# Hymba step: the scan's half of the output projection as 2x2x2 block products, with the factors of the scan's outputs built behind each group's norm

## The chip, the cores and the metric

The kernel runs on one core of a Trainium2 chip. The metric is the time of one execution in device microseconds (us). The engines are named as the profile names them: PE (TensorE, matrix products), DVE (VectorE), ACT (ScalarE), POOL (GpSimd) and SP (SyncE, which issues the DMAs). A line number L1040 is a line of the kernel that the row belongs to.

## What is computed

One step of a decoder layer with 1024 channels over T = 1088 tokens (1024 of a prompt, and 8 sequences of 8). The part that the change touches is the mixer and its output projection:

```python
h = rmsnorm(x, g_mix_pre) * (1 + scale_m) + shift_m
proj = h @ w_in
sc_b, sc_c, sc_x, z, xbc, dt_raw = jnp.split(proj, idx, axis=-1)
...
y_sc = sc_b * uc
...
yg = (y_ssd * jax.nn.silu(z)).reshape(bsz, L, SSM_GROUPS, SSM_WIDTH // SSM_GROUPS)
y_ssd = rmsnorm(yg, 1.0).reshape(bsz, L, SSM_WIDTH) * ssm_norm_g
mix = jnp.concatenate([y_sc, y_ssd], axis=-1) @ w_out
x = x + gate_m * rmsnorm(mix, g_mix_post)
```

`uc` is the causal convolution of `sc_c * sc_x`; `y_ssd` is the output of a scan in four groups of 256 channels. So `w_out` has 2048 rows: 1024 for the short convolution's half (`y_sc`) and 1024 for the scan's half (`y_ssd`). After the mixer comes a feed-forward block, which the change leaves alone.

## The kernel before, in words

**Numbers.** Every fp32 matrix is held as a sum of two reduced-precision parts, hi (a cast on ACT) and lo (value minus hi, a subtraction on DVE). A product is three matmuls: hi by hi, hi by lo, lo by hi. `split` (L298 cast, L299 subtraction) does this for a whole row of 1088 tokens, `part` (L1039, L1040) for a block.

**Layout.** Activations lie with channels on the 128 partitions and the 1088 tokens along the row. A row tile is 128 x 1088, 557 KB. A scan group g has two such tiles, `y[0]` and `y[1]`.

**Block products.** Where the kernel multiplies blockwise it cuts both factors 2x2: seven products of blocks in place of eight, after sums and differences of blocks of both factors. `unit` (L1082 on) issues the seven in the order 1, 5, 6, 3, 7, 2, 4. For each it queues its matmuls (`product`, L1078 to L1080) into a PSUM tile `pm` for the first half of tokens (q = 0) and `pz` for the second, then takes the sum out with ACT (`nc.scalar.copy`, L1093) where it opens an output, or DVE (an addition, L1095) where it adds to one. Product 6 adds on top of product 1 in the same PSUM tile, and product 3 on top of product 5, so each must wait until the copy of the earlier sum has been made. A unit of the short convolution has 7 x 24 = 168 matmuls of 272 columns. Such units make the short convolution's input columns (`sc_unit`), and the down projection of the feed-forward block.

**The order of the work.** Program order is written out by hand, with generators that are advanced between steps: `between={n: [gen]}` of a unit advances `gen` once behind its n-th product; `merge(a, b, ratio)` advances b by `ratio` steps for each step of a. A layer then decides from the program order and the buffers where an instruction stands in each engine's queue; each engine runs its queue in order. What matters here is this sequence:

1. The scan of group 3 (`ssd`, to about 450 us). Beside it run the gates and norms of groups 0 and 1 as side work, `merge(..., 1.67)`.
2. The late gates of groups 2 and 3 (`gate_late`, L1165, 470 to 515 us).
3. Twelve units of the short convolution, three for each of four pairs of channel tiles: two input columns' units (`cc`, `cx`), then the convolution of the pair on DVE (L1209, L1210, L422 to L429), then the third unit (`cb`). Unit 3, from about 554 us, is the third unit of the first pair; unit 4 is the first of the second pair. Norms of groups 2 and 3 are advanced between the products of these units.
4. The scan's half of the output projection (770 to 867 us), the short convolution's half behind it.

**The norm of a scan group** (`norm`, L913) computes sums of squares (ACT squares, PE sums), scales the two row tiles on DVE (L939), and then splits each tile: hi goes into a new row buffer, lo stays in place, and both go to DRAM (`y_out`, L948 to L950, tensors `y_d`). For groups 0 and 1 the row buffers come from `fm_row`, a pool with eight of them; for groups 2 and 3 from `sx_row` (L1177):

```python
pap, psx, psy = (pool(left, n, b) for n, b in (("pap", 2), ("psx", 1), ("psy", 1)))
```

So `psx` has a single buffer.

**The scan's half before** (L1277 to L1297) is a plain product. Sixteen row tiles (hi and lo of 8) are loaded into `fx`, `btp` and `h2p`; for each of 4 x 2 column tiles of the weights and each of three pieces of the tokens (512, 304, 272) eight k-tiles of three matmuls are summed (L334 to L336), 576 matmuls in all, and ACT copies the sum into the accumulators `acc`.

Of the kernel before, what the change touches and what calls it, by code (L numbers as in the profile page):

```python
# [9 lines left out]
F32 = mybir.dt.float32  # L10
# [6 lines left out]
P = 128  # L17
D = 1024
# [15 lines left out]
def hymba_step(ctx, tc, i, o):  # L34
# [877 lines left out]

    def norm(g, y, new_sq, new):  # L913

        ps = pz()
        sq = []

        def sums(c):
            for j in range(3):
                mm(ps[:, 3 * c + j:3 * c + j + 1], sq[c][:, 0, j * P:(j + 1) * P], ones[:, 0:1],  # L920
                   start=(c == 0 and j == 0), stop=(c == 2 and j == 2))

        for c, (c0, n) in enumerate(CH):
            q = new_sq()
            sq.append(q)
            if n < 384:
                nc.gpsimd.memset(q[:, 0, n:384], 0.0)
            for m in range(2):
                nc.scalar.square(q[:, m, :n], y[m][:, c0:c0 + n])
            nc.vector.tensor_tensor(q[:, 0, :n], q[:, 0, :n], q[:, 1, :n], op=add)  # L930
            sums(c)
            yield
        r = rsqrt_of(ps[:, 0:9], 2 * P)
        yield
        for c, (c0, n) in enumerate(CH):
            rs = spread(r[:, 3 * c:3 * c + 3], n)
            for m in range(2):
                v = y[m][:, c0:c0 + n]
                nc.vector.scalar_tensor_tensor(v, v, sng[:, 2 * g + m:2 * g + m + 1], rs, op0=mult, op1=mult)  # L939
# [27 lines left out]
    def fm_row():  # L967
        return fmp.tile([P, T], F32, tag="fm", name=nm("nr"))

    def blend(a, b, na, nb):  # L970
# [19 lines left out]
    for g in range(4):  # L990
        if g < 3:
            side = group_tiles(g + 1, tl[g + 1])
            if g > 0:
                side = blend(side, ada_steps(g), 12, 9)
        else:
            gates, norms = zip(*((gate(h, tl[h][:2]), norm(h, tl[h][:2], lambda: gz([P, 2, 384]), fm_row))
                                 for h in range(2)))
            side = itertools.chain(gates[0], norms[0], gates[1], load_next(), norms[1])
        run(merge(ssd(g, *tl[g], load_later if g == 3 else None), side, (0.67, 1.17, 1.17, 1.67)[g]))
    pre_scale("A_f", 4, gpre1)  # L1000
# [36 lines left out]

    def part(hi, lo, v, eng=None):
        nc.scalar.copy(hi, v)  # L1039
        (eng or nc.vector).tensor_tensor(lo, v, hi, op=sub)  # L1040

    def combos_w(w, cols, eng=nc.gpsimd):
# [39 lines left out]
    def unit(W, X, nk, qs, out, first=True, between={}, blocks_=QS, queue=in_order):  # L1082
# [3 lines left out]
        for n, (p, b, new, i, h, opens) in enumerate(ORDER):  # L1086
            for q in qs:
                if new:
                    B[b, q] = (pm, pz)[q]()
                ps = B[b, q][:, :blocks_[q][1]]  # L1090
                queue(product, ps, W[p], X[q][p], nk, new, p in (3, 2, 4))
                if first and opens:
                    nc.scalar.copy(out(q, i, h), ps)  # L1093
                else:
                    nc.vector.tensor_tensor(out(q, i, h), out(q, i, h), ps, op=add)  # L1095
            for gen in between.get(n, ()):
# [101 lines left out]
    for pr in range(4):  # L1198
# [77 lines left out]

    first = []  # L1277
    for k in range(KT):
        v = [(fx, btp, h2p)[(k > 3) + (k > 5)].tile([P, T], F32R, tag="bt" if k in (4, 5) else "fm", name=nm("hb"))
             for _ in range(2)]  # L1280
        first.append(v)
    for cols in (slice(0, 512), slice(512, T)):
        for k in range(KT):
            for e in range(2):
                nc.sync.dma_start(first[k][e][:, cols].bitcast(F32), y_d[8 + k][:, e, cols])
    for mp in range(4):
        for m, (wh, wl) in enumerate(load_cols(w_out, mp * 256, 2, D)):
            for c0, n in OC:
                ps = pm()
                acc3(ps, n, [(wh[:, k, :], wl[:, k, :], first[k][0][:, c0:c0 + n], first[k][1][:, c0:c0 + n])  # L1290
                             for k in range(KT)])
                nc.scalar.copy(acc_at(2 * mp + m, c0, n), ps[:, :n])
        if mp == 0:
            while kept:
                y_out(*kept.pop(0))
        if mp == 2:
            in_order(conv_state, nsc, 8, 2, o["scc_p"], o["scc_s"])  # L1297


    def out_split(c):  # L1300
        c0, n = OC[c]
        terms = []
        for k in range(KT):
            if c < 2:
                hb = ((fa if k < 4 else fb) if c == 0 else fx).tile([P, 2, n], F32R, tag="fm", name=nm("hb"))
            elif k % 2 == 0:
                hb2 = bt_([P, 2, 2, n], F32R)
# [331 lines left out]
    def combos_d(g, mp, eng):  # L1639
        nk = len(g)  # L1640
        raw = raws_d.pop(0) if raws_d else raw_d(g, mp)
        A = raw.rearrange("p (k j) (i c) -> p i j k c", j=2, i=2)
        a11, a12, a21, a22 = (A[:, m, j] for m in range(2) for j in range(2))
        W = {}


        pair = [in_turn(w_from).tile([P, 2, 2, 2, P], F32R, tag="wc", name=nm("wd")) for _ in range(4)]

        def parts_(p, b):
            n = (1, 5, 6, 3, 7, 2, 4).index(p)  # L1650
            t = pair[n // 2][:, n % 2]
            part(t[:, 0], t[:, 1], b)
            W[p] = [[t[:, s, k] for k in range(nk)] for s in range(2)]

        parts_(1, a11)
        parts_(4, a22)
        eng.tensor_tensor(a22, a21, a22, op=add)
        parts_(5, a22)
        eng.tensor_tensor(a21, a11, a21, op=sub)
        eng.tensor_tensor(a11, a22, a11, op=sub)  # L1660
        parts_(6, a11)
        parts_(2, a12)
        eng.tensor_tensor(a12, a12, a11, op=sub)
        parts_(3, a12)
        parts_(7, a21)
        return W

# [128 lines left out]
```

## Time and profile before

| | |
|---|---|
| runs | 1731.94, 1732.16, 1736.8 us; median 1732.16 |
| the profiled execution | 1732.75 us, span from the first to the last instruction 1731.0 us |
| granted PE clock, mean over the span | 0.990 |
| busy: PE, DVE, ACT, POOL | 97%, 66%, 45%, 11% of the span |
| DMA | 256.37 MB, mean 148 GB/s |

How to read it: the busy share of PE is that of a queue with work in it; matmuls are pipelined, and the end of one is modelled. So the time that a stretch of matmuls needs is read from its length and its count, not from the sum of their durations. A row of the windows view gives a stretch's length, then each engine's busy time with its number of instructions, the granted PE clock, the busy share of the DMA engines and GB/s. A row of the timeline gives start, duration, engine, line, operation, output, inputs and, in brackets, how long the engine sat idle before it and what released it.

### The profile page before, as it was taken

The page shows a single profiled execution, that of the slowest core. Times are in us where ns is not written, and L with a number is a line of the kernel's source. Part 1 is how long each engine was busy: PE and PEld are TensorE (multiplying, and loading weights), DVE is VectorE, ACT ScalarE, POOL GpSimd, SP SyncE. Part 2 cuts the span into 40 slices and gives each one's busy share as a digit, 9 for nine tenths or more (in the row PEclk, how much of TensorE's full clock was granted, in tenths as well). Part 3 has the DMA queues.
Part 4 walks back from the last instruction along what each step waited for, and adds up shares of the span by engine and source line. Part 5 has one row for each costly group of instructions (what it writes and reads, how often), then busy time and mean ns, then how long its engine had stood idle before and what let it go on. Part 6 is the DMA issues. An engine that isn't in the chain of part 4 may idle for free. (4 is left out here: it accounts for less than half of the span.)

```text
span 1731.0 us, 31270 instructions
## 1 busy us (share of the span) xinstructions
PE 1682.0 (97%) x12604; PEld 1600.0 (92%) x12604; DVE 1147.9 (66%) x2194; ACT 770.9 (45%) x1571; POOL 185.7 (11%) x277
## 2 busy tenths in 40 slices
PE   5999999999999999999999999999999999999997
PEld 4898888899999999998989999999999999999987
DVE  5588677777798776661037779666666658588734
ACT  3457454657544433322226676444444446422222
POOL 2110001000001000000000000122222200122112
PEclk9999999999999999999999999999999999999999
DMA  9201344442322522348275643334433438865523
GB/s 321 73 21 30 113 152 151 148 131 77 109 69 77 177 70 74 113 165 301 69 255 183 195 134 140 121 140 142 147 131 140 148 123 312 314 230 198 203 92 134
DMA packets 159624, 256.37 MB, mean 148 GB/s; under 512 B 10578, under 2 KB 123394, under 8 KB 157943
## 3 DMA queue, kind: packets, MB, share of 16 engines
q1 hardware_dynamic: 159190, 253.19, 42.9%
q8 instruction: 99, 1.62, 0.4%
q10 hardware_dynamic: 288, 1.18, 0.2%
q14 instruction: 47, 0.38, 0.1%
HBM read 184.63 MB, written 69.71 MB: 147 GB/s over the span
## 5 line engine op out<-in xcount | busy, mean ns | idle before, releaser
L312 DVE TENSOR_TENSOR wl<-raw,wh 128x512 fp32r<-128x512 f32 (+1 forms) x87 | 61.3, 729 | 100.3 <-ACT wh L311 89.2
L334 PE MATMUL pm<-h,wh 128*128 128x384 f32 (+1 forms) x342 | 115.1, 337 | 0.1
L335 PE MATMUL pm<-h,wh 128*128 128x384 f32 (+1 forms) x342 | 114.9, 336 | 0.0
L336 PE MATMUL pm<-h,wl 128*128 128x384 f32 (+1 forms) x342 | 114.3, 335 | 0.0
L336 PE MATMUL pm<-hb,wl 128*128 128x512 f32 (+2 forms) x320 | 107.3, 337 | 2.1 <-DVE wl L312 2.1
L311 ACT CAST wh<-raw 128x512 fp32r<-128x512 f32 (+1 forms) x89 | 56.4, 665 | 116.2 <-PE pm L335 68.2
L335 PE MATMUL pm<-hb,wh 128*128 128x512 f32 (+2 forms) x320 | 107.4, 337 | 0.0
L334 PE MATMUL pm<-hb,wh 128*128 128x512 f32 (+2 forms) x320 | 105.8, 338 | 1.0 <-ACT wh L311 1.0
L1039 ACT CAST wd<-raw 128x256 fp32r<-128x256 f32 x112 | 42.9, 406 | 96.1 <-PE pz L1080 33.6
L1040 DVE TENSOR_TENSOR fs<-f,fs 128x576 fp32r<-128x576 f32 (+2 forms) x76 | 52.9, 710 | 25.3 <-ACT fs L1039 24.5
L336 PEld LDWEIGHTS pm<-hb,wl 128*128 128x128 f32 x320 | 60.8, 190 | 7.6 <-DVE wl L312 2.4
L334 PEld LDWEIGHTS pm<-h,wh 128*128 128x128 f32 x342 | 65.5, 191 | 1.9 <-issue 0.9
L335 PEld LDWEIGHTS pm<-h,wh 128*128 128x128 f32 x342 | 65.3, 191 | 1.4 <-issue 0.7
L334 PEld LDWEIGHTS pm<-hb,wh 128*128 128x128 f32 x320 | 60.3, 190 | 6.8 <-ACT wh L311 1.2
L336 PEld LDWEIGHTS pm<-h,wl 128*128 128x128 f32 x342 | 65.2, 191 | 1.3 <-issue 1.0
L1078 PE MATMUL pz<-fc,wd 128*128 128x288 f32 x224 | 66.2, 295 | 0.0
L1080 PE MATMUL pz<-fc,wd 128*128 128x288 f32 x224 | 66.0, 295 | 0.0
L1079 PE MATMUL pz<-fc,wd 128*128 128x288 f32 x224 | 65.9, 294 | 0.0
L335 PEld LDWEIGHTS pm<-hb,wh 128*128 128x128 f32 x320 | 60.8, 190 | 5.2
L1078 PE MATMUL pm<-fc,wd 128*128 128x256 f32 x224 | 63.3, 283 | 1.4 <-DVE facc L1095 1.4
L1040 DVE TENSOR_TENSOR wd<-raw,wd 128x256 fp32r<-128x256 f32 x112 | 54.4, 494 | 14.6 <-ACT wd L1039 14.2
L1080 PE MATMUL pm<-fc,wd 128*128 128x256 f32 x224 | 63.1, 282 | 0.3 <-DVE wd L1040 0.3
(5568 smaller groups left out, 6203.2 us busy)
## 6 DMA issues: line engine op xcount, KB each, us to landing
raw<-in_w_in SPq DMA_DIRECT2D x48, 512.0 KB
wa<-in_w_ada SPq DMA_DIRECT2D x32, 512.0 KB
raw<-in_w_out SPq DMA_DIRECT2D x32, 512.0 KB
f_d<-fs SPq DMA_DIRECT2D x28, 576.0 KB
f_d<-fs SPq DMA_DIRECT2D x30, 512.0 KB
raw<-in_w_gate SPq DMA_DIRECT2D x28, 512.0 KB
raw<-in_w_up SPq DMA_DIRECT2D x28, 512.0 KB
y_d<-y SPq DMA_DIRECT2D x26, 544.0 KB
```

Of the source, the lines that this page charges most:

```text
L311: (nc.gpsimd.tensor_copy if hi_eng else nc.scalar.copy)(wh, raw)
L312: (eng or nc.vector).tensor_tensor(wl, raw, wh, op=sub)
L334: mm(ps[:, :n], wh, xh, start=(first and j == 0), stop=False)
L335: mm(ps[:, :n], wh, xl, start=False, stop=False)
L336: mm(ps[:, :n], wl, xh, start=False, stop=(last and j == end))
L1039: nc.scalar.copy(hi, v)
L1040: (eng or nc.vector).tensor_tensor(lo, v, hi, op=sub)
L1078: mm(ps, W[0][k], X[0][k], start=(start and k == 0), stop=False, skip_group_check=True)
L1079: mm(ps, W[0][k], X[1][k], start=False, stop=False, skip_group_check=True)
L1080: mm(ps, W[1][k], X[0][k], start=False, stop=(stop and k == nk - 1), skip_group_check=True)
```

## The change

The scan's half of the output projection becomes eight units of block products: two pairs of scan groups (groups 0 and 1, groups 2 and 3) by four pairs of column tiles of the weights, each 7 products x 12 matmuls of 272 columns, 672 matmuls in all. The second pair adds to the accumulators with DVE, where the first opens them with ACT. Each unit's weights are cut and combined (`combos_p`, shared now with the down projection) with sums on DVE for the first pair and on POOL for the second.

The block sums of the scan's outputs are made once, behind each group's norm. `factors_out` makes seven factors from the four blocks of a group; each has 128 x 544 elements, hi and lo lie side by side in one row buffer, and one DMA stores it (`yx_d`, 28 of 557 KB in place of 16 stores). For groups 0 and 1 two factors are made a step, with rows from the eight of `fm_row`, and the ratio of `merge` is 1.88 in place of 1.67. For groups 2 and 3 every factor's row comes from `sx_row`, one factor a step; the third unit of a pair now advances the norms once behind each product, before twice; factors of group 2 and the norm of group 3 advance together. Loads of the factors take 14 rows for each pair of groups. `conv_state` and the last stores of the short convolution move behind unit 0 of the eight, from between the columns of the plain product.

```diff
-        for m in range(2):
-            hi = new()[:, :T].bitcast(F32R)
-            lo = y[m].bitcast(F32R)
-            split(hi, lo, y[m])
-            y_out(8 + 2 * g + m, hi, lo)
-            yield
+    def factors_out(g, y, new):
+        (b11, b12), (b21, b22) = blocks_h(y[0]), blocks_h(y[1])
+        def put(p, b):
+            t = new()[:, :T].bitcast(F32R).rearrange("p (s q n) -> p s q n", s=2, q=2)
+            part(t[:, 0], t[:, 1], b)
+            nc.sync.dma_start(yx_d[g][p - 1].rearrange("p s (q n) -> p s q n", q=2), t.bitcast(F32))
+        put(1, b11)
+        yield
...
+        nc.vector.tensor_tensor(b11, b12, b11, op=sub)
+        put(5, b11)
+        yield
+        nc.vector.tensor_tensor(b12, b22, b12, op=sub)
+        put(7, b12)
+        yield
+        nc.vector.tensor_tensor(b22, b22, b11, op=sub)
+        put(6, b22)
+        yield
+        nc.vector.tensor_tensor(b21, b21, b22, op=sub)
+        put(4, b21)
+        yield
...
-            gates, norms = zip(*((gate(h, tl[h][:2]), norm(h, tl[h][:2], lambda: gz([P, 2, 384]), fm_row))
+            gates, norms = zip(*((gate(h, tl[h][:2]), itertools.chain(
+                norm(h, tl[h][:2], lambda: gz([P, 2, 384])), by_twos(factors_out(h, tl[h][:2], fm_row))))
...
-    norms = itertools.chain(*(norm(g, ys[g], sq_row, sx_row) for g in (2, 3)))
+    def norms_():
+        yield from norm(2, ys[2], sq_row)
+        for _ in zip(factors_out(2, ys[2], sx_row), norm(3, ys[3], sq_row)):
+            yield
+        yield from factors_out(3, ys[3], sx_row)
...
-        sc_unit(256 * pr, cb, {n: [norms, norms] for n in range(7)})
+        sc_unit(256 * pr, cb, {n: [norms] for n in range(7)})
...
+    F = factors_in((0, 1), [fx] * 8 + [btp] * 4 + [h2p] * 2)
+    for n in range(8):
+        pr, mp = n // 4, n % 4
+        W = combos_p(raws_o.pop(0), w_tile, 2, (nc.vector, nc.gpsimd)[pr])
+        unit(W, F, 2, [0, 1], acc_blocks(mp), pr == 0, {}, SQ)
+        if n == 0:
+            in_order(conv_state, nsc, 8, 2, o["scc_p"], o["scc_s"])
+            while kept:
+                y_out(*kept.pop(0))
+            F2 = factors_in((2, 3), [h2p] * 2 + [fb] * 6 + [yp4] * 4 + [yp2] * 2)
```

The change moves instructions on every engine. Two places are shown, both where unit 3 runs. First ACT's queue of before, from the last unit's final copies on: `y_5258` is an output of unit 2, `y_5798` and `y_5799` are those of unit 3, `w__...` are weights, `sq_` are squares for the norm of group 3. In brackets is what an instruction waits for, DMAHW being a DMA.

```order
L1093 COPY y_5258<-pm_5541 128x272 [waits PE_49]
L1093 COPY y_5258<-pz_5555 128x272 [waits PE_49]
L929 ACTIVATE sq_5857<-y_3198 128x320 [waits DVE_49,PE_49]
L929 ACTIVATE sq_5857<-y_3400 128x320
L1093 COPY y_5798<-pm_5829 128x272 [waits DMAHW5_49,PE_49]
L1093 COPY y_5798<-pz_5843 128x272 [waits PE_49]
L1039 CAST w__751_6087<-raw_6082 128x512 [waits DMAHW1_49]
L1093 COPY y_5799<-pm_5878 128x272 [waits DVE_49,PE_49]
```

The same place of ACT's queue now: `y_5322` is the output of unit 2, `y_5890` and `y_5891` are those of unit 3. `y_5808`, `y_5847`, `y_5950`, `y_5989` and `y_6026` are the rows of factors 3, 5, 7, 6 and 4 of group 2, each in the one buffer of `psx`.

```order
L1156 COPY y_5322<-pm_5605 128x272 [waits PE_49]
L920 CAST y_5808<-y_2535 128x544 [waits DMAHW1_49,DVE_49]
L1156 COPY y_5322<-pz_5619 128x272 [waits PE_49]
...
L920 CAST y_5847<-y_2333 128x544 [waits DMAHW3_49,DVE_49]
L920 CAST y_5950<-y_2333 128x544 [waits DMAHW5_49,DVE_49,Activation_49]
L920 CAST y_5989<-y_2535 128x544 [waits DMAHW6_49,DVE_49]
L1156 COPY y_5890<-pm_5921 128x272 [waits DVE_49]
L1156 COPY y_5890<-pz_5935 128x272
...
L920 CAST y_6026<-y_2535 128x544 [waits DMAHW7_49,DVE_49,Activation_49]
L1156 COPY y_5891<-pm_5960 128x272 [waits DVE_49]
```

Three factors' casts, each with a wait for a DMA, now stand between the last copy of unit 2 and the first copy of unit 3, where only squares stood, and a fourth stands ahead of the copy of unit 3's second product.

Second, DVE's queue of before beside unit 2's end and unit 3's start. `y_5698` is the last hi row of group 2, `y_5257` an output of unit 2, `y_5772` the product that the first pair's convolution (L1209 on) works on.

```order
L299 TENSOR_TENSOR y_2515<-y_2515,y_5698 128x1088 [waits Activation_49]
L1095 TENSOR_TENSOR y_5257<-y_5257,pm_5703 128x272 [waits PE_49]
L1210 TENSOR_TENSOR y_5772<-y_5255,y_5257 128x8x8 [waits DMAHW3_49,DVE_49]
L1040 TENSOR_TENSOR w__750_6084<-raw_6080,w__750_6084 128x512 [waits DMAHW0_49,Activation_49]
L423 TENSOR_SCALAR y_5255<-y_5772,vT 128x64 [waits DVE_49,Pool_49]
```

DVE's queue now, with the subtractions of factors 7 (`y_5950`) and 6 (`y_5989`), and the convolution (`y_5864`, `y_5877`; L1275 on):

```order
L921 TENSOR_TENSOR y_5950<-y_2333,y_5950 128x544 [waits DMAHW5_49,Activation_49]
L1091 TENSOR_TENSOR raw_6173<-raw_6173 128x4x128 [waits DVE_49]
L1275 TENSOR_TENSOR y_5864<-y_5319,y_5321 128x1024 [waits DVE_49]
L1276 TENSOR_TENSOR y_5864<-y_5319,y_5321 128x8x8
L424 TENSOR_SCALAR y_5319<-y_5864,vT 128x1024 [waits DVE_49,Pool_49]
...
L430 SCALAR_TENSOR_TENSOR y_5320<-y_5877,vT,y_5320 128x1024 [waits DVE_49]
L431 SCALAR_TENSOR_TENSOR y_5320<-y_5877,vT,y_5320 128x64 [waits DVE_49]
L921 TENSOR_TENSOR y_5989<-y_2535,y_5989 128x544 [waits DMAHW6_49,Activation_49]
```

Before, all of group 2's splitting stood ahead of the convolution; now the convolution of the pair stands between the subtractions of factors 7 and 6.

More of the change, by code (lines that the diff above doesn't have):

```diff
@@ L911, in gate_out, with blocks_h, part, norm @@
         return evac
-    def norm(g, y, new_sq, new):
+    def blocks_h(v):
+        v = v.rearrange("p (q h n) -> p q h n", q=2, h=2)
+        return v[:, :, 0], v[:, :, 1]
+    def part(hi, lo, v, eng=None):
+        nc.scalar.copy(hi, v)
+        (eng or nc.vector).tensor_tensor(lo, v, hi, op=sub)
+    def norm(g, y, new_sq):
         ps = pz()
@@ L968, in fm_row, with by_twos @@
         return fmp.tile([P, T], F32, tag="fm", name=nm("nr"))
+    def by_twos(gen):
+        for _ in gen:
+            next(gen, None)
+            yield
     def blend(a, b, na, nb):
@@ L1061, in combos_w, with combos_p, parts_ @@
         nc.vector.tensor_tensor(a12, a12, a11, op=sub)
+        parts_(3, a12)
+        parts_(7, a21)
+        return W
+    def combos_p(raw, new, nk, eng):
+        A = raw.rearrange("p (k j) (i c) -> p i j k c", j=2, i=2)
+        a11, a12, a21, a22 = (A[:, m, j] for m in range(2) for j in range(2))
+        W = {}
+        pair = [new() for _ in range(4)]
+        def parts_(p, b):
+            n = (1, 5, 6, 3, 7, 2, 4).index(p)
+            t = pair[n // 2][:, n % 2]
+            part(t[:, 0], t[:, 1], b)
+            W[p] = [[t[:, s, k] for k in range(nk)] for s in range(2)]
+        parts_(1, a11)
+        parts_(4, a22)
+        eng.tensor_tensor(a22, a21, a22, op=add)
+        parts_(5, a22)
+        eng.tensor_tensor(a21, a11, a21, op=sub)
+        eng.tensor_tensor(a11, a22, a11, op=sub)
+        parts_(6, a11)
+        parts_(2, a12)
+        eng.tensor_tensor(a12, a12, a11, op=sub)
         parts_(3, a12)
@@ L1274, in acc_at, with factors_in @@
         return acc[q][:, m, c0 - QS[q][0]:c0 - QS[q][0] + n]
[L1277 to L1293, printed above, removed]
+    def factors_in(gs, places):
+        places = iter(places)
+        F = [{} for _ in SQ]
+        for p in (1, 5, 6, 3, 7, 2, 4):
+            tiles = []
+            for g in gs:
+                pl = next(places)
+                t = yt(pl, dt=F32R) if pl in (yp4, yp2) else pl.tile(
+                    [P, T], F32R, tag="bt" if pl is btp else "fm", name=nm("yx"))
+                nc.sync.dma_start(t.bitcast(F32), yx_d[g][p - 1].rearrange("p s n -> p (s n)"))
+                tiles.append(t.rearrange("p (s q n) -> p s q n", s=2, q=2))
+            for q in range(2):
+                F[q][p] = [[t[:, s, q] for t in tiles] for s in range(2)]
+        return F
@@ new lines, in hymba_step, with w_tile, acc_blocks, out @@
+    turns = [0]
+    def w_tile():
+        n, turns[0] = turns[0], turns[0] + 1
+        pl, tag = (wp, ("wh", "wl")[n % 2]) if n // 4 % 2 == 0 else (fa, "fm")
+        return pl.tile([P, 2, 2, 2, P], F32R, tag=tag, name=nm("wo"))
+    def acc_blocks(mp):
+        def out(q, i, h):
+            c0, n = SQ[q][0] + 272 * h, 272
+            ends = [c0, 512, c0 + n] if c0 < 512 < c0 + n else [c0, c0 + n]
+            return [(acc_at(2 * mp + i, a, b - a), slice(a - c0, b - c0)) for a, b in zip(ends, ends[1:])]
+        return out
@@ L1639, in combos_d @@
     def combos_d(g, mp, eng):
[L1640 to L1666, printed above, removed]
+        return combos_p(raws_d.pop(0) if raws_d else raw_d(g, mp), lambda: in_turn(w_from).tile(
+            [P, 2, 2, 2, P], F32R, tag="wc", name=nm("wd")), len(g), eng)
     for j in range(2):
```

38 lines of the change are left out of this document (23 added, 15 removed).

## The prediction

> **What bounds the kernel now.** First the page's busy times.
>
> ```profile
> span 1731.0 us, 31270 instructions
> PE 1682.0 (97%) x12604; PEld 1600.0 (92%) x12604; DVE 1147.9 (66%) x2194; ACT 770.9 (45%) x1571; POOL 185.7 (11%) x277
> ```
>
> PE is at work nearly throughout. So a change is worth the PE time it removes, less the idle time it puts between matmuls. Second, PE in the stretches at stake (columns: length, then PE, PEld, DVE, ACT, POOL, granted clock, DMA share, GB/s): the scan's half of the output projection, then two units of block products of the short convolution, 168 matmuls of 272 columns each.
>
> ```profile
> 770.70:866.60 95.90, 94.91 (x576) 86.08 (x575) 14.62 (x20) 20.99 (x43) 0.00 (x0) 1.00 0.56 200
> 579.00:600.10 21.10, 21.10 (x170) 21.10 (x169) 15.35 (x23) 9.72 (x18) 0.40 (x2) 1.00 0.67 236
> 600.10:621.20 21.10, 21.10 (x171) 21.10 (x170) 10.70 (x22) 5.17 (x12) 1.16 (x5) 1.00 0.09 26
> ```
>
> All three are bound by PE. A 272-column matmul costs 21.10 / 168 = 0.1256 us, and 24 of them, a product, 3.0 us.
>
> Third, the two places where the new work is put. In the next fence are the scan's last group and the scan's late gates, where groups 0 and 1 are normed, and a pause of PE with what followed it.
>
> ```profile
> 421.00:430.00 9.00, 9.00 (x71) 8.02 (x70) 7.95 (x16) 8.92 (x18) 0.00 (x0) 1.00 0.62 248
> 430.00:440.00 10.00, 10.00 (x79) 8.75 (x78) 8.04 (x24) 9.84 (x17) 0.00 (x0) 1.00 0.01 2
> 490.00:500.00 10.00, 10.00 (x61) 10.00 (x60) 9.58 (x15) 4.37 (x8) 0.00 (x0) 1.00 0.00 0
> 500.00:510.00 10.00, 8.92 (x66) 8.47 (x65) 10.00 (x17) 4.96 (x11) 0.00 (x0) 1.00 0.00 0
> 510.00:520.00 10.00, 9.02 (x57) 8.80 (x58) 8.75 (x16) 4.33 (x9) 0.00 (x0) 0.83 0.35 107
> 512.25:515.66 3.41, 3.41 (x17) 3.41 (x16) 3.41 (x6) 0.76 (x2) 0.00 (x0) 0.50 0.70 207
> ```
>
> From 490 to 516 DVE, not PE, sets the pace: DVE is full while PE idles 1.08 and 0.98 us. After the idling PE ran one window of 3.41 us at clock 0.50.
>
> **Part 1, the block products.** 576 matmuls in 95.90 us become 8 units x 84 = 672 of 272 columns: 672 x 0.1256 = 84.4 us, 11.5 us less. Their DVE work (7 subtractions, up to 4 sums and 14 additions or copies a unit) is that of the down projection, built from the same units; there PE never waits:
>
> ```profile
> 1520.00:1600.00 80.00, 80.00 (x641) 80.00 (x640) 66.48 (x161) 21.28 (x55) 21.92 (x30) 1.00 0.54 202
> ```
>
> The start is tighter. Before, the loads of the scan's outputs ran from 754.85 at 346 GB/s:
>
> ```profile
> 754.85 25.48 SPq L1285 DMA_DIRECT2D hb<-y_d  x32
> 760.00:780.00 20.00, 20.00 (x134) 18.65 (x133) 10.03 (x14) 4.93 (x8) 0.00 (x0) 1.00 0.98 346
> ```
>
> Now 14 loads of 557 KB (7.8 MB, 22.5 us at that rate, done about 778) feed unit 0, whose seven products of 1.5 us begin at 770.7, so the last starts at 779.7. I take 1 us for the start, between 0 and 9. **Term 1: -10.5 (-11.5 to -2.5).**
>
> **Part 2, factors of groups 0 and 1.** Durations, ACT's cast and then DVE's operations:
>
> ```profile
> 473.21 0.65 ACT L1039 CAST x__636_4870<-y 128x544 fp32r<-128x544 f32 x1
> 541.72 1.11 ACT L298 CAST y<-y 128x1088 fp32r<-128x1088 f32 x1 [0.35 <-DVE y L939]
> 474.19 0.72 DVE L1040 TENSOR_TENSOR x__636_4870<-y,x__636_4870 128x544 fp32r<-128x544 f32 x1
> 469.80 0.72 DVE L1144 TENSOR_TENSOR y<-y 128x544 f32<-128x544 f32 x1
> 543.01 1.28 DVE L299 TENSOR_TENSOR y<-y,y 128x1088 fp32r<-128x1088 f32 x1
> ```
>
> A group has 2 casts and 2 subtractions of 1088 removed, and 7 casts, 7 subtractions and 4 block sums of 544 added: DVE 11 x 0.72 - 2 x 1.28 = +5.4 us, ACT 7 x 0.65 - 2 x 1.11 = +2.3 us. Group 1's 5.4 us falls where DVE is full and goes to the end one for one. Group 0's falls where DVE has 3.0 us free in 19; about 1.6 of the rest shows. **Term 2: +7** (+2 if DVE catches up before the first products that need its sums; +11 if neither is hidden). The 14 stores a group rotate over several buffers; I cost them at nothing, covered by the 0.01 DMA share at 430 to 440.
>
> **Part 3, factors of groups 2 and 3.** Here all fourteen rows pass through one buffer (pool psx), so a factor's cast waits until the store of the one before has landed, and ACT runs its queue in order. Two stores of 557 KB before, by their issue, and what moved behind them, bear on a landing:
>
> ```profile
> 548.31 0.32 SPq L949 DMA_DIRECT2D y_d<-y  x1
> 549.64 0.32 SPq L950 DMA_DIRECT2D y_d<-y  x1
> 548.30:548.90 0.60, 0.60 (x7) 0.60 (x7) 0.58 (x1) 0.52 (x1) 0.39 (x2) 1.00 0.00 0
> 548.90:550.40 1.50, 1.50 (x16) 1.50 (x14) 1.50 (x4) 0.20 (x1) 1.01 (x2) 1.00 0.86 351
> 550.40:552.00 1.60, 1.60 (x14) 1.60 (x15) 1.56 (x6) 1.30 (x3) 0.35 (x1) 1.00 0.92 367
> ```
>
> Nothing moves for 0.6 us, then 557 KB at 359 GB/s take 1.55: at least 2.15 us. From above, a cast held by such a store, and ACT's queue at the next one:
>
> ```profile
> 542.85 0.34 SPq L949 DMA_DIRECT2D y_d<-y  x1
> 547.19 1.10 ACT L298 CAST y<-y 128x1088 fp32r<-128x1088 f32 x1 [2.37 <-DMA y_d<-y]
> 577.75 0.39 ACT L1093 COPY y<-pm 128x272 f32<-128x272 f32 x1 [0.88 <-PE pm L1080]
> 579.90 1.10 ACT L298 CAST y<-y 128x1088 fp32r<-128x1088 f32 x1 [1.77 <-DVE w__756_6106 L1040]
> 580.91 0.38 ACT L1093 COPY y<-pz 128x272 f32<-128x272 f32 x1
> ```
>
> 547.19 - 542.85 = 4.34 us. I take 2.75, nearer the bound below, since the second store's bytes were all moved 2.4 us after its issue. By the Trainium skill, "DMA: Bandwidth & Descriptors", section "Anatomy of one DMA", a DMA has a fixed cost of about 2.0 us, most of it the write's receipt, beside its bytes at 436 GB/s: an estimated 3.3 us here, with which this part would be some 4 us dearer; that fit is for another issue path, and the rows above hold 3.3 between their ends. The last two rows show the harm already: the evacuation at 580.91, due 1.5 us after 577.75, stood behind the cast.
>
> A round is cast 0.65 + subtraction 0.72 + landing 2.75 = 4.1 us, while a step of the program is one product of 3.0 us. In ScalarE's new order three such casts (factors 5, 7, 6 of group 2) stand ahead of the first evacuation of the third unit, and the cast of factor 4 ahead of that of its second product; in unit 4 likewise. The rest needs unit 3's clock before and DVE's convolution:
>
> ```profile
> 554.10:579.00 24.90, 24.41 (x195) 24.03 (x195) 23.66 (x49) 8.93 (x18) 2.21 (x5) 1.00 0.26 86
> 552.37 0.39 ACT L1093 COPY y<-pm 128x272 f32<-128x272 f32 x1 [0.67 <-PE pm L1080]
> 556.05 0.39 ACT L1093 COPY y<-pm 128x272 f32<-128x272 f32 x1 [0.79 <-PE pm L1080]
> 557.55 0.39 ACT L1093 COPY y<-pz 128x272 f32<-128x272 f32 x1 [1.11 <-PE pz L1080]
> 551.64 1.22 DVE L1209 TENSOR_TENSOR y<-y,y 128x1024 f32<-128x1024 f32 x1
> 553.25 0.75 DVE L422 TENSOR_SCALAR y<-y,vT 128x1024 f32<-128x1024 f32 x1
> 554.05 1.28 DVE L428 SCALAR_TENSOR_TENSOR y<-y,vT,y 128x1024 f32<-128x1024 f32 x1
> 559.61 0.27 DVE L429 SCALAR_TENSOR_TENSOR y<-y,vT,y 128x64 f32<-128x64 f32 x1
> ```
>
> Unit 3, on before's clock: its first half product is evacuated at 556.05 and took 1.5, so it starts at 554.5. Its third product (block product 6) needs the PSUM tile of the first; it is due at 554.5 + 6.0 + 0.9 for the norm's small matmuls (an estimate: a quarter of 24.90 - 21.10) = 561.4. Factor 3's cast follows the evacuation at 552.37, so it starts at 552.8. Three rounds of 4.1, and an estimated 1.5 in which the subtractions stand behind the norm's small operations, put factor 6's cast at 566.7; with it (0.65) and the evacuation (0.39) the product starts at 567.7, **6.3 us late**. Factor 6's subtraction stands in DVE's order behind the whole convolution of the pair, 2 x (1.22 + 0.75 + 2 x 1.28 + 4 x 0.27), less overlap, about 9.8 us, which starts when factor 7's subtraction is through (563.9). So it ends at 563.9 + 0.4 + 9.8 + 0.7 = 574.8, lands at 577.6, and the cast of factor 4 and the evacuation behind it end at 578.6. The fourth product was due at 570.7: **7.9 late**. Four products on, the unit ends at 590.7; before, the next began at 579.0: +11.6.
>
> Unit 4, from its start U: factor 3's subtraction stands behind four operations on 1088 elements for unit 3's result (about 5.2 us) and ends at U + 5.9. Landing, cast, subtraction, landing, cast, evacuation: U + 13.85, due at U + 6.0: **7.8 late**. The cast of factor 6, one more round, factor 4's cast: U + 22.1, due at U + 16.9: **5.2 late**. So +13.0, and for both +24.5. Eight landings lie on that path: at 2.36 it is 21, at 4.34 it is 37; if PE's pauses let DVE run ahead of what I assume, I put the least at 19.
>
> SyncE's queue holds each store until its subtraction is done, and loads of the fifth unit's weights stand behind those of group 3; they are a unit early, which covers it. If not, that unit would start some 3 us late.
>
> Each of these four stops is over 3.41 us, so half-clock windows like the one at 512.25 follow: each costs PE up to 1.7 us, none to four of them (0 to 7); since a window may begin inside the stop, I take 3. The Trainium skill, "TensorE: Matmul & The Clock Gate", Part 1, has the rule: after an idle window of about 3.4 us the array runs at half rate until a busy window has passed. By that rule the full 7 would come if every stop ended at a window's start; the 0.50 over 3.41 us here agrees with it. **Term 3: +24.5 + 3 = +27.5 (+19 to +44).**
>
> **The sum** against the profiled execution (span 1731.0, with 1.75 us around it 1732.75): 1732.75 - 10.5 + 7 + 27.5 = 1756.75. It lies 0.6 above the median 1732.16, so I forecast **1756**. Its own range, not all ends at once: 1742 to 1774.
>
> **Rivals.**
> 1. *The rounds are hidden, only the matmuls count (faster).* For it: before, the evacuation at 580.91 came some 1.7 us late, and PE was busy for all 21.10 us of 579.00:600.10. Against: there one such cast stood between, now three in a row. Term 3 nothing, term 2 at 2: 1732.2 - 11.5 + 2 = 1723. It decides where the rounds end before 561.4, that is 7.6 us for three, a landing of about 1.1 us, and the convolution is out of the way too.
> 2. *One stop in four (even).* The first stop gives DVE some 6 us, in which the convolution and the next subtractions run ahead, so that the other three close up. One stop of 8, term 2 at 2: 1732.2 - 10.5 + 2 + 8 = 1732.
> 3. *The new units start on loads that are not there (slower still).* Unit 0 takes two factors every 1.5 us while 1.1 MB needs 3.2: if the buffers come free at 770 and not from 755, it is paced by them, 7 x 1.7 = up to 12 us more: 1768. Against: the 0.98 DMA share shows before's loads well under way by then.
>
> **How the numbers follow.** Forecast 0.70, rival 1 0.14, rival 2 0.08, rival 3 0.08. About 0.3%, 5 us, is what a measurement of this kernel can tell from no change. Faster 0.14, same 0.08, slower 0.78. A range from 1731 to 1774 leaves out rival 1 and about 0.05 above.
>
> **What would show it.** In the changed profile: the scan half in 84 to 86 us; four PE stops of 5 to 8 us released by ACT or PSUM evacuations in the third and fourth units after the late gates (about 555 to 640), ACT waiting there on the stores of the factors, with clock 0.5 behind; the late gates' end some 5 us later with DVE full. The prediction is wrong if those two units still take 25 and 21 us.

## The result, and the profile after

| | before | changed |
|---|---|---|
| median of the runs | 1732.05 us (4 runs, 1729.13 to 1736.8) | 1774.79 us (4 runs, 1771.55 to 1776.46) |
| span of the profiled execution | 1731.0 us | 1771.4 us |

The ratio is 1.0241, with a 95% interval of 1.0221 to 1.0260: by the medians the change makes the kernel 43 us slower, where 24 were forecast. The forecast was 1756 us; the result lies at the upper end of its range, 1774: the median is 0.8 us above it, the ratio times the median of 1732.16 is 1773.9.

The page of the changed kernel, beside the one above:

```profile
span 1771.4 us, 31873 instructions
PE 1689.0 (95%) x12700; PEld 1610.1 (91%) x12700; DVE 1220.1 (69%) x2390; ACT 790.9 (45%) x1647; POOL 197.8 (11%) x293
```

PE has 96 matmuls more and is busy 7 us longer, in a span that is 40 us longer: the time is in pauses and in matmuls at half clock. The windows view says where. The rows are the scan's half of the projection, unit 3, unit 4, and the time right after unit 3's first stop:

```profile
813.90:907.50 93.60, 88.29 (x682) 85.64 (x682) 66.35 (x179) 35.26 (x102) 12.46 (x17) 1.00 0.84 301
565.45:605.63 40.18, 26.40 (x188) 25.99 (x187) 31.48 (x54) 11.63 (x22) 3.62 (x8) 0.83 0.36 130
605.63:643.26 37.63, 25.66 (x170) 25.22 (x169) 19.30 (x28) 11.32 (x22) 0.24 (x2) 0.82 0.45 169
583.40:586.80 3.40, 3.36 (x16) 3.36 (x17) 3.40 (x7) 0.53 (x2) 0.34 (x1) 0.57 0.00 0
```

The projection's half took 95.90 us before (770.70 to 866.60) and takes 93.6 now, 2.3 less. Unit 3 took 24.8 us and takes 40.2; unit 4 took 21.1 and takes 37.6: 32.0 us more for the two. Unit 3 starts at 565.45 where it started at 554.25: 11.2 us more by then. With 0.5 us less behind the projection, 11.2 + 32.0 - 2.3 - 0.5 = 40.4 us, the difference of the two spans.

What PE waited for from 555 to 645, by the waits view (us in total, times, longest):

```profile
PE pm L1139 <- ACT y L1156: 25.8, 4, 9.8
```

Four stops, 25.8 us (9.8, 3.95, 8.5 and 3.5), all released by ScalarE's copies out of PSUM. The other 6.2 of the 32.0 us are matmuls at half clock behind them, as at 583.40: 66 matmuls there start 0.227 us apart in place of 0.126.

Next, ScalarE around those stops, from the timeline: casts of factors (L920) and copies (L1156). Behind it SyncE's row for the store ahead of the first cast shown.

```profile
573.96 0.65 ACT L920 CAST y<-y 128x544 fp32r<-128x544 f32 x1 [3.99 <-DMA yx_d<-y]
578.94 0.65 ACT L920 CAST y<-y 128x544 fp32r<-128x544 f32 x1 [4.34 <-DVE y L425]
583.00 0.39 ACT L1156 COPY y<-pm 128x272 f32<-128x272 f32 x1 [3.41 <-DVE y L1276]
...
591.52 0.39 ACT L1156 COPY y<-pm 128x272 f32<-128x272 f32 x1 [0.79 <-DVE y L921]
...
618.40 0.64 ACT L920 CAST y<-y 128x544 fp32r<-128x544 f32 x1 [3.68 <-DMA yx_d<-y]
619.83 0.39 ACT L1156 COPY y<-pm 128x272 f32<-128x272 f32 x1 [0.79 <-DVE y L921]
...
628.23 0.39 ACT L1156 COPY y<-pm 128x272 f32<-128x272 f32 x1 [0.82 <-DVE y L921]
```

```profile
571.18 0.32 SPq L959 DMA_DIRECT2D yx_d<-y  x1
```

The cast at 573.96 starts 2.78 us after the issue of the store before it: the landing that the prediction took at 2.75. But look at 583.00. The cast at 578.94 was over at 579.6, and ScalarE then sat idle for 3.41 us before the copy. So it was not the cast in the queue that held this copy; it waited for DVE. At the other three the cast ends only 0.8 us before the copy, so there the timeline alone hardly tells the two apart. DVE's timeline, first the subtraction of factor 7 of group 2 and the start of the convolution, then the operations at the four copies:

```profile
575.43 0.72 DVE L921 TENSOR_TENSOR y<-y,y 128x544 fp32r<-128x544 f32 x1
...
576.67 1.22 DVE L1275 TENSOR_TENSOR y<-y,y 128x1024 f32<-128x1024 f32 x1
...
582.75 0.22 DVE L1276 TENSOR_TENSOR y<-y,y 128x64 f32<-128x64 f32 x1
...
590.76 0.72 DVE L921 TENSOR_TENSOR y<-y,y 128x544 fp32r<-128x544 f32 x1
...
619.07 0.73 DVE L921 TENSOR_TENSOR y<-y,y 128x544 fp32r<-128x544 f32 x1 [1.96 <-ACT y L920]
...
627.48 0.72 DVE L921 TENSOR_TENSOR y<-y,y 128x544 fp32r<-128x544 f32 x1
```

Each copy starts within 0.1 us of the end of one of the last four. A copy reads a PSUM sum, which PE makes, and writes one tile; so what it waits for on DVE is the tile. At 582.75 the convolution reads an output of unit 2 for the last time, in a tile that unit 3 then writes; the convolution itself stands in DVE's queue behind the subtraction of factor 7 (575.43). The others are subtractions of factor 4 of group 2 and of factors 7 and 4 of group 3, each the last read of a row tile of its group. This gives the theory that the experiments test, called **lifetime**: the outputs of units 3 and 4 are written into tiles (pools `yp4` and `yp2`) that the scan's outputs of groups 2 and 3 hold or, for the first copy, an output of unit 2 that the convolution has yet to read. A row tile comes free when the last factor that reads it has been made, and the chain of rounds through the one row buffer says when that is. The rival is the step as the prediction put it: the copies stand behind the casts in ScalarE's **queue**. Under both a copy comes after the casts, so the order alone does not tell them apart.

The earlier delay, 11.2 us at unit 3's start, begins in the scan's last group:

```profile
440.00:450.00 10.00, 6.81 (x34) 6.25 (x32) 9.41 (x16) 7.89 (x16) 0.00 (x0) 0.83 0.20 52
450.00:460.00 10.00, 10.00 (x103) 8.44 (x101) 3.91 (x10) 2.00 (x4) 0.15 (x1) 0.66 0.21 71
460.00:470.00 10.00, 10.00 (x56) 9.90 (x55) 5.38 (x17) 1.23 (x3) 0.00 (x0) 0.83 0.16 50
```

PE pauses for 3.2 us within 440 to 450, and the granted clock is low in all three rows. But the kernel before, which had no pause, was below full clock over 450 to 460 too:

```profile
450.00:460.00 10.00, 10.00 (x77) 9.38 (x76) 5.12 (x18) 1.06 (x2) 0.00 (x0) 0.83 0.34 108
453.90:457.30 3.40, 3.40 (x14) 3.40 (x13) 2.44 (x14) 0.47 (x1) 0.00 (x0) 0.55 0.50 154
```

In the changed kernel the low clock comes in two stretches. Behind the pause the matmuls are slow from 446.4 to 449.8; from 450 to 452 the clock is 1.00; then, behind a run of small matmuls, it is low again for some 10 us:

```profile
453.00:456.50 3.50, 3.50 (x26) 3.15 (x22) 0.48 (x3) 0.73 (x2) 0.00 (x0) 0.53 0.02 5
456.50:460.00 3.50, 3.50 (x38) 2.61 (x37) 2.51 (x6) 0.44 (x1) 0.00 (x0) 0.50 0.02 7
460.00:463.40 3.40, 3.40 (x13) 3.38 (x12) 0.86 (x5) 0.47 (x1) 0.00 (x0) 0.50 0.47 147
```

### The profile page after: what moved, and what is told of

Its sections match the earlier page's. It is cut to its first block, busy times and chain, and to the rows that moved or that the text cites. A ratio compares the mean times of both kernels' runs of the same rounds, so it can differ in the third digit from the quotient of the medians.

```text
span 1771.4 us, 31873 instructions
## 1 busy us (share of the span) xinstructions
PE 1689.0 (95%) x12700; PEld 1610.1 (91%) x12700; DVE 1220.1 (69%) x2390; ACT 790.9 (45%) x1647; POOL 197.8 (11%) x293
## 4 chain that ended last, share of the span: by engine, by line
PE 78%; DVE 9%; DMA 6%; ACT 3%; issue 2%; SPq 1%; POOL 1%; DVEq 0%; ACTq 0%; POOLq 0%
PE pm L336 8%; PE pm L338 8%; PE pm L337 8%; PE pz L1139 7%; PE pz L1141 7%; PE pz L1140 7%; PE pm L1141 7%; PE pm L1139 7%; PE pm L1140 7%; PE pm L211 1%; DMA raw<-in_w_up 1%; PE pz L753 1%; DMA yx<-yx_d 1%; DMA f_d<-fs 1%; PE pz L747 1%
## 5 line engine op out<-in xcount | busy, mean ns | idle before, releaser
L313 ACT CAST wh<-raw 128x512 fp32r<-128x512 f32 (+1 forms) x73 | 46.6, 674 | 116.3 <-PE pm L337 69.6
L920 ACT CAST wd<-raw 128x256 fp32r<-128x256 f32 x112 | 42.7, 406 | 95.9 <-PE pz L1141 33.7
L1139 PE MATMUL pm<-fc,wd 128*128 128x256 f32 x224 | 63.4, 283 | 1.5 <-DVE facc L1158 1.0
L1141 PE MATMUL pm<-fc,wd 128*128 128x256 f32 x224 | 63.3, 283 | 0.3 <-DVE wd L921 0.3
L920 ACT CAST fs<-f 128x576 fp32r<-128x576 f32 (+2 forms) x76 | 44.5, 599 | 42.5 <-DMA f_d<-fs 23.7
L1140 PE MATMUL pm<-fc,wd 128*128 128x256 f32 x224 | 62.9, 281 | 0.0
L314 DVE TENSOR_TENSOR wl<-raw,wh 128x512 fp32r<-128x512 f32 (+1 forms) x71 | 50.3, 739 | 14.2 <-ACT wh L313 11.3
L336 PE MATMUL pm<-bt,wh 128*128 128x384 f32 (+2 forms) x146 | 51.4, 352 | 2.0 <-ACT wh L313 2.0
L1158 DVE TENSOR_TENSOR facc<-facc,pz 128x288 f32<-128x288 f32 x96 | 43.2, 450 | 12.4 <-PE pz L1141 12.3
L338 PE MATMUL pm<-bt,wl 128*128 128x384 f32 (+1 forms) x146 | 48.6, 333 | 1.6 <-DVE wl L314 1.6
L1158 DVE TENSOR_TENSOR facc<-facc,pm 128x256 f32<-128x256 f32 x96 | 39.8, 415 | 13.5 <-PE pm L1141 12.0
```

Source lines behind the costliest of these rows:

```text
L313: (nc.gpsimd.tensor_copy if hi_eng else nc.scalar.copy)(wh, raw)
L314: (eng or nc.vector).tensor_tensor(wl, raw, wh, op=sub)
L336: mm(ps[:, :n], wh, xh, start=(first and j == 0), stop=False)
L338: mm(ps[:, :n], wl, xh, start=False, stop=(last and j == end))
L1139: mm(ps, W[0][k], X[0][k], start=(start and k == 0), stop=False, skip_group_check=True)
L1140: mm(ps, W[0][k], X[1][k], start=False, stop=False, skip_group_check=True)
```

## The experiments

Each is compared with the kernel before on its own chip (medians there 1730.9 to 1733.4 us); a ratio to it stands with its interval. Those medians lie up to 2.4 us apart, so a difference of 2 or 3 us between two runs says little.

**The factors of groups 2 and 3 left out** (with `F2 = factors_in((0, 1), ...)`):

```diff
-        for _ in zip(factors_out(2, ys[2], sx_row), norm(3, ys[3], sq_row)):
-            yield
-        yield from factors_out(3, ys[3], sx_row)
+        yield from norm(3, ys[3], sq_row)
```

> The changed kernel without making and storing the factors of groups 2 and 3; their half of the projection reads the factors of groups 0 and 1 instead, so the output is not the reference's. It sizes the third term: in the changed kernel's trace units 3 and 4 take 40.2 and 37.6 us where they took 24.8 and 21.1, +32 us in all. If those stops are all that the factors of groups 2 and 3 cost: 1775 - 32 = 1743 us (1740 to 1746). If they also cost DVE time elsewhere, or hid something that now appears: outside that.

Measured 1742.21 us, ratio 1.0056 (1.0038 to 1.0073). PE's only wait from 555 to 640 is now this one:

```profile
PE pz L293 <- DVE sm L287: 1.4, 1, 1.4
```

The stops of units 3 and 4 are gone, and 32.6 us with them, about the 32.0 of the two units. So little else in the kernel pays for those factors.

**Every store of groups 2 and 3 twice.**

```diff
-            nc.sync.dma_start(yx_d[g][p - 1].rearrange("p s (q n) -> p s q n", q=2), t.bitcast(F32))
+            for to in ([yx_d[g][p - 1]] if g < 2 else [yx_d[g][p - 1], again_d[g][p - 1]]):
+                nc.sync.dma_start(to.rearrange("p s (q n) -> p s q n", q=2), t.bitcast(F32))
```

> The changed kernel, with every factor of groups 2 and 3 stored twice, the second time to a tensor that nobody reads; the single row buffer comes free only when both stores have landed. A store's bytes took 1.55 us, so each landing gets about 1.5 us later. Theory 1 (the chain of rounds through the one buffer sets the stops in units 3 and 4): eight landings on that path, +12 us, 1787 us (1782 to 1792). Rival (the added work of DVE and ACT sets them): no change within 2 us, 1775.

Measured 1791.68 us, ratio 1.0342 (1.0326 to 1.0358). The waits view, from 555 to 670:

```profile
PE pm L1142 <- ACT y L1159: 41.0, 4, 15.7
```

The same four stops, 41.0 us in place of 25.8, though no engine computes anything more. So the landings lie on the path that sets the stops; the work of DVE and ScalarE is at most a part of it. (The total is at the upper end of what was expected. About 3.5 us of it arose before unit 1, where the added stores play no part: unit 1 starts at 514.14. In the runs here whose program is the changed kernel's up to there, it starts anywhere from 508.56 to 514.14.)

**Casts of groups 2 and 3 on GpSimd**, which takes them out of ScalarE's queue:

```diff
+        cast = nc.gpsimd.tensor_copy if g > 1 else nc.scalar.copy
...
-            part(t[:, 0], t[:, 1], b)
+            cast(t[:, 0], b)
+            nc.vector.tensor_tensor(t[:, 1], b, t[:, 0], op=sub)
```

> The changed kernel with the casts of the factors of groups 2 and 3 on GpSimd instead of ScalarE, so that no cast stands ahead of a copy out of PSUM in ScalarE's queue; the one row buffer and the tiles are as they were. Rival (ScalarE's queue holds the copies): the stops of units 3 and 4 go, 1775 - 27 = 1748 us. Theory 1 (lifetime of the tiles, with the chain of rounds): the copies wait for the last factor all the same, 1775 us, up to 5 us more where GpSimd's cast is slower than ScalarE's 0.65 us (1772 to 1782).

Measured 1775.96 us, ratio 1.0255 (1.0235 to 1.0275), as lifetime expects; the queue falls as the cause of the stops. ScalarE's copies and PE's waits in that kernel:

```profile
584.52 0.39 ACT L1158 COPY y<-pm 128x272 f32<-128x272 f32 x1 [13.67 <-DVE y L1278]
...
594.39 0.39 ACT L1158 COPY y<-pm 128x272 f32<-128x272 f32 x1 [2.64 <-DVE y L960]
...
621.24 0.39 ACT L1158 COPY y<-pm 128x272 f32<-128x272 f32 x1 [3.58 <-DVE y L960]
...
630.18 0.39 ACT L1158 COPY y<-pm 128x272 f32<-128x272 f32 x1 [2.43 <-DVE y L960]
```

```profile
PE pm L1141 <- ACT y L1158: 25.5, 4, 9.8
```

ScalarE sat idle for 13.67 us with nothing ahead of the copy in its queue, and the copy still came with DVE's release: 25.5 us of stops, as with the casts in the queue (25.8).

**Half the pace.**

```diff
         for _ in zip(factors_out(2, ys[2], sx_row), norm(3, ys[3], sq_row)):
             yield
-        yield from factors_out(3, ys[3], sx_row)
+            yield
+        for _ in factors_out(3, ys[3], sx_row):
+            yield
+            yield
```

> The changed kernel with the factors of groups 2 and 3 made at half the pace, one per two products (6 us) in place of one per product. Rival, as the prediction had it (ScalarE's queue: the copies out of PSUM stand behind casts that come faster than a round of 4.1 us): the rounds fit, the stops go, 1775 - 25 = 1750 us. Theory 1 (lifetime: the outputs of units 3 and 4 are written into tiles that the scan's outputs of groups 2 and 3 hold until their last factor is made): the last factors come later, five rounds in place of two are left in unit 4, 3 x 4.3 us more, 1788 us (1782 to 1794).

Measured 1788.91 us, ratio 1.0324 (1.0308 to 1.0339). The waits view, from 555 to 665:

```profile
PE pm L1139 <- ACT y L1156: 35.0, 4, 20.2
```

Giving each round twice the time made it 14 us slower, which only lifetime expected: the longest stop, now 20.2 us, is at unit 4, where more factors of group 3 are left to be made.

**Two half rows in the same buffer.**

```diff
+            if new is None:
+                for q in range(2):
+                    t = psh.tile([P, 2, T // 4], F32R, tag="yh", name=nm("yh"))
+                    part(t[:, 0], t[:, 1], b[:, q])
+                    nc.sync.dma_start(yx_d[g][p - 1].rearrange("p s (q n) -> p s q n", q=2)[:, :, q], t.bitcast(F32))
+                return
```

> The changed kernel with the one row buffer of groups 2 and 3 cut into two halves of the same size together: each factor goes out as two stores of half the bytes (0.78 us of bytes each), one in flight while the other half is cast and subtracted. Theory 1 (the chain of rounds sets when the tiles come free): a round falls from 4.1 us to some 2.8 for a factor, so of 27 us of stops about half stay, 1760 us (1752 to 1766). If the last factors' place behind the pair's convolution in DVE's queue sets it, whatever a round takes: 1772 us or more.

Measured 1771.59 us, ratio 1.0221 (1.0202 to 1.0240): a miss, and the alternative that was written beside it came nearer. Units 3 and 4 took 34.85 and 35.58 us, 7.4 less than in the changed kernel; but the first unit started 4.1 us later (514.78 against 510.68), little beyond the spread of that start between runs. PE's stops in the two units are 19.4 us in place of 25.8:

```profile
PE pm L1145 <- ACT y L1162: 19.4, 4, 6.8
```

So shorter rounds help less than in proportion. The small DVE operations ahead of each subtraction, and the convolution, are part of the chain too, and each half row has a landing of its own; no run says which of these counts most.

**The norms 15 us earlier.**

```diff
-        sc_unit(1024 + 256 * pr, cc, {n: [norms] for n in range(3, 7)})
+        sc_unit(1024 + 256 * pr, cc, {n: [norms, norms] if pr == 0 and n < 4 else [norms] for n in range(7)})
```

> The changed kernel with the norms and factors of groups 2 and 3 begun five products (15 us) earlier: advanced twice behind the first four products of the first unit, and in all of its products. Theory 1 (lifetime): the chain of fourteen rounds of 4.1 to 4.3 us then ends before the outputs of unit 4 need the tiles, and its first half before unit 3's do; the stops of units 3 and 4 and their half-clock windows go, 1775 - 30 = 1745 us (1742 to 1752). Rival (DVE's load): the same work only moves to where DVE is full at 500 to 520 us already, 1770 us or more.

Measured 1770.08 us, ratio 1.0214 (1.0196 to 1.0231): a miss by 25 us. PE's waits from 500 to 640:

```profile
PE pz L930 <- DVE sq L940: 13.8, 1, 13.8
PE pm L1139 <- ACT y L1156: 4.4, 1, 4.4
```

The lifetime part did what was expected: 25.8 us of stops became 4.4. But the norm's sums of squares now stand in PE's queue in unit 1, before DVE gets to them, and cost 13.8 us at one stroke, with half clock behind. Here DVE's load is the price, as the rival said.

**All three mends together**: half rows, two steps of the norms behind the last product of unit 1 and the first of unit 2, the fifth unit's weights first (below).

> The changed kernel with three edits that leave all its work in: two half rows in the buffer of groups 2 and 3, their norms advanced twice behind the last product of unit 1 and the first of unit 2 (so the factors start 6 us earlier), and the fifth unit's weights loaded first. Theory 1 (lifetime): both halves of the chain get shorter or earlier by 6 to 12 us, so that of 32 us at units 3 and 4 at most 8 are left; with 5 us from the weights 1775 - 24 - 5 = 1746 us (1741 to 1753). If the place of the last factors behind the convolution, or DVE's load, sets it: 1762 us or more.

Measured 1759.23 us, ratio 1.0160 (1.0135 to 1.0185), between the two expectations. Unit 3 takes 28.8 us (24.8 before), unit 4 33.5 us (21.1 before). ScalarE at unit 4's two longest stops:

```profile
605.38 0.39 ACT L1162 COPY y<-pm 128x272 f32<-128x272 f32 x1 [1.31 <-DVE yh L921]
...
614.77 0.39 ACT L1162 COPY y<-pm 128x272 f32<-128x272 f32 x1 [0.51 <-DVE yh L921]
```

They are still released by the subtractions of group 3's last factors. PE's stops in the two units are 13.5 us. Unit 3 is nearly mended, unit 4 is not; the second seven rounds follow the first seven through the same buffer, which is the likely reason. No run moved unit 4's outputs to other tiles, so that last step, the tiles themselves, is shown by the releases and by the runs above, and not by an edit of its own.

**The fifth new unit's weights first.**

```diff
+            raws_o.append(raw_o(4))
             F2 = factors_in((2, 3), [h2p] * 2 + [fb] * 6 + [yp4] * 4 + [yp2] * 2)
-        if n < 4:
+        if 0 < n < 4:
             raws_o.append(raw_o(n + 4))
```

> The changed kernel with the load of the fifth new unit's weights issued ahead of the fourteen loads of the second pair's factors, not behind them. In the changed kernel's trace GpSimd's first sum for that unit waits for this load until 861.5 us, and PE loses about 5.5 us from 859 to 879. Theory 3 (the load is late): -4 us, 1771 us (1769 to 1773). Rival (GpSimd's sums and DVE, busy 18.3 of 24.1 us there, set it): within 1 us of 1775.

In the changed kernel, GpSimd's first sum for that unit, and the window around it (150 matmuls, 18.8 us at 0.1256, in 24.1):

```profile
861.55 0.85 POOL L1116 TENSOR_TENSOR raw<-raw 128x256 f32<-128x256 f32 x1 [65.20 <-DMA raw<-in_w_out]
```

```profile
855.90:880.00 24.10, 21.07 (x150) 19.02 (x149) 18.30 (x50) 8.61 (x24) 9.32 (x12) 1.00 0.99 340
```

The DMA share is 0.99: the weights came in behind fourteen factors. With them first, the projection's half:

```profile
812.70:902.90 90.20, 86.25 (x683) 85.20 (x682) 65.16 (x179) 34.84 (x102) 12.35 (x17) 1.00 0.83 295
```

It takes 90.2 us in place of 93.6, and the kernel 1769.45 us, ratio 1.0215 (1.0194 to 1.0236). The load was late, as expected; by the stretch itself that was worth 3.4 us. The totals differ by 5.3, but unit 1, long before the edit, already started 2.1 us earlier in this run.

**The factors of groups 0 and 1 left out** (`norm` alone in the side work, `F = factors_in((2, 3), ...)`):

> The changed kernel without making and storing the factors of groups 0 and 1; their half of the projection reads those of groups 2 and 3, so the output is not the reference's. It sizes the second term by itself. In the changed kernel the first unit starts at 510.7 where it started at 502.2, and the third 11.2 us later than before. If that whole delay is the factors of groups 0 and 1: 1775 - 11 = 1764 us (1761 to 1767). If only their group 1 on a full DVE counts (5.4 us, as predicted): 1769.

Measured 1765.28 us, ratio 1.0191 (1.0166 to 1.0217): 9.5 us less by the medians, 5.9 by the profiled spans (1765.5). Its windows where the changed kernel paused:

```profile
440.00:450.00 10.00, 10.00 (x63) 9.66 (x62) 8.08 (x21) 9.71 (x20) 0.00 (x0) 1.00 0.33 105
450.00:460.00 10.00, 10.00 (x86) 9.25 (x86) 7.89 (x17) 4.18 (x7) 0.15 (x1) 1.00 0.01 2
460.00:470.00 10.00, 10.00 (x121) 8.88 (x120) 7.36 (x19) 1.07 (x2) 0.00 (x0) 1.00 0.04 13
```

No pause, and the clock at 1.00. So the pause at 442 to 446 comes with these factors, and the low clock too, beyond the one stretch that the kernel before has. Whether the low clock after 453 is due to the pause isn't shown. Unit 1 starts at 501.94, 8.7 us earlier than in the changed kernel; but there PE then waits 4.1 us for DVE (a subtraction for its weights), and unit 3 starts at 558.31, only 7.1 earlier and still 4.1 later than before. So not all of the 11.2 us goes with the factors. (The run keeps the ratio of 1.88 of `merge`; its share was not measured.)

**Casts of groups 0 and 1 on GpSimd** (as above, with `g < 2`):

> The changed kernel with the casts of the factors of groups 0 and 1 on GpSimd instead of ScalarE. In the changed kernel's trace PE first stops at 442 to 446 us, released by ScalarE's cast of the gate's weights, ScalarE is busy 9.9 of 10 us from 420 to 440, and the clock is 0.83, 0.66 and 0.83 behind it. Theory 2 (ScalarE's load sets term 2): that stop and its half-clock windows go, -6 us, 1769 us (1766 to 1771). Rival (DVE's load sets it, as predicted): no change within 2 us, 1775.

Measured 1778.82 us, ratio 1.0266 (1.0250 to 1.0282): no gain (the median is 4 us higher, but the intervals overlap), and theory 2 falls as written. The pause remains, now released by DVE, from 430 to 520:

```profile
PE pm L338 <- DVE wl L314: 3.8, 1, 3.8
```

But the edit isn't neutral to DVE. GpSimd's cast and the DVE sum beside it (its form's median over 32 is 0.69 us), and an earlier sum, of a form that takes 0.72 us elsewhere:

```profile
435.41 0.97 POOL L959 CAST nr<-fm 128x544 fp32r<-128x544 f32 x1 [3.52 <-DVE fm L978]
```

```profile
435.80 1.12 DVE L739 TENSOR_TENSOR st<-st,fm 128x512 f32<-128x512 f32 x1
429.59 1.16 DVE L975 TENSOR_TENSOR fm<-fm,fm 128x544 f32<-128x544 f32 x1
```

So it can't settle whether DVE alone would have been enough; that stays open.

**The block products alone**, no factors for any group (the units read rows of other stores), weights first:

> The block products alone: no factors are made for any group, the units read rows of the short convolution's stores instead (the output is not the reference's), and the weights of the fifth unit are loaded first, as in the run with that change. It sizes the first term without what feeds it. 672 matmuls of 0.1256 us are 84.4 us, with some 3 us at the start and 1 us behind it 88.5, where the plain product took 95.6: 1733 - 7 = 1726 us (1723 to 1729). If the units' own DVE and GpSimd work or their loads cost what they save: 1731 us or more.

Measured 1729.22 us, ratio 0.9995 (0.9982 to 1.0009). No difference can be measured, where 7 us were expected. The stretch itself:

```profile
770.90:861.10 90.20, 86.25 (x683) 85.19 (x682) 65.14 (x179) 34.70 (x102) 12.33 (x17) 1.00 0.83 296
```

It is 5.7 us shorter than the plain product, and the profiled span is 3.9 us shorter (1727.1); of that the runs, which scatter over 8 us, leave between 3 us of gain and 2 us of loss. So with its factors for nothing this change would have been worth a few microseconds at best.

## Why the prediction was right, and where it was off

- **The sign and its cause** were right: slower, because the factors of groups 2 and 3 go through one buffer round by round. The landing was 2.78 us against the 2.75 taken. The four stops were forecast at 6.3, 7.9, 7.8 and 5.2 us, 27.2 in sum; the waits row has 25.8. The size was not right: 24 us were forecast and 43 measured.
- **The step that was wrong in term 3** is what a copy waits for. The prediction read ScalarE's order and said that the copies stand behind the casts. They wait for the tile they write (583.00 and its 3.41 us of idling; the run with the casts on GpSimd, unchanged at 1775.96). The cast of factor 6, put at 566.7 on the old clock, 577.9 with the 11.2 us, came at 578.94; the copy came not behind it but 4 us later. The sum came out because both say "not before the last factors"; as far as this step goes that was luck. The split didn't: the first stop is 9.8 us and not 6.3, since its copy waits for more than half of the convolution, and the next is 3.95 and not 7.9, since by then less of it was left. A mend built on the queue would have failed, as the casts on GpSimd did.
- **The clock's part of term 3** was mis-sized: 3 us were taken, about 6 measured (32.0 - 25.8), near the upper end of 7.
- **Term 2** was mis-sized and put in the wrong place: +7 forecast, 11.2 at unit 3's start, 9.5 when taken out. The prediction had group 1 pay 5.4 us in the late gates and group 0 only 1.6. By the starts of the late gates' matmuls 6.9 of the 11.2 us were there at 469.60 (462.72 before), as group 1's first factor was being cast (469.25), and 8.0 by the second half of the late gates. So most of it came with group 0, as a pause of 3.2 us and more half clock than before. For group 0 the prediction read DVE's 3.0 us of free time, but not that ScalarE had none (8.92 of 9 and 9.84 of 10 in the same rows), and it put a pause and the clock at nothing there; which engine's load made the pause stays open. The other 4.3 us are near the 5.4 taken for group 1, but they aren't shown to be its own: without the factors unit 3 still started 4.1 us late. (The late gates' matmuls end at 502.18 in the kernel before, where unit 1 starts, and not at about 515.)
- **Term 1** was mis-sized: -10.5 forecast, -2.3 in the changed kernel, just outside its own end of -2.5. The matmuls cost what was said. The start lost some 2.5 us, with PE waiting for sums of the weights and not for the loads that the prediction feared; the fifth unit's stretch lost some 5, of which its late weights were 3.4, a queue that the prediction named only for the first pair's loads. And what the stretch gains isn't all seen at the end: alone it is worth 0 to 3 us.
- With term 2 at 11.2, term 3 at 32.0 and term 1 at -2.3, the sum is 1732.75 + 40.9 = 1773.7 by the prediction's own account.
- **The rivals.** None of the three stands as written. The rounds were not hidden, all four stops came, and the first unit did not wait 12 us for its loads.

## What to carry to other kernels

When a step is made longer, ask what else lives in its tiles: here the largest part of the price was set by the next user of a buffer, waiting for its old owner's last read. An engine's order shows that something waits, and the released-by column of the timeline shows on what; an idle engine ahead of the waiting instruction rules the queue out. Before counting matmuls saved, measure the product with its inputs for nothing: here that alone would have shown a few microseconds to be won.

## What the runs showed of the hardware

PE can count as busy in the profile and still run at half clock. Behind the first stop of unit 3, which ended at 583.4, dense matmuls of 272 columns followed, and the low stretch was 3.4 us at 0.57. The Trainium skill, "TensorE: Matmul & The Clock Gate", Part 1, asks for a sustained busy window of about 3.4 us before full rate returns; this row agrees with it. Behind the pause at 442 the clock came back as soon, but with small matmuls it fell again: 0.53 over 453.00 to 456.50 and 0.50 from there to 463.40, with PE busy for all of it. The kernel before fell to 0.55 over 453.90 to 457.30 without a pause. So half clock can come without a pause. Small matmuls stand in or just ahead of both stretches and are the likely cause, but that isn't shown: the run without the factors of groups 0 and 1 had many of them too (121 matmuls from 460 to 470), at a clock of 1.00.

GpSimd's casts can slow DVE: two two-input DVE operations that ran beside them, of forms that take 0.69 and 0.72 us elsewhere, took 1.12 and 1.16. The Trainium skill, "SBUF — State Buffer", section "Who interferes with whom", says that a DVE instruction with both inputs in SBUF contends with a GpSimd instruction that reads SBUF; the rows agree.
